# ACT's rounding of weight tiles is queued behind the evacuation three products back, and the two ends of the attention are reordered

## The chip, the core and the metric

The kernel runs on one core of one Trainium2 chip. PE is the matmul engine, with PEld its weight loads; DVE, ACT and POOL are the vector, scalar and GpSimd engines; SP issues nearly all DMAs. Each engine works through its own queue in the order in which the program was laid down for it. The metric is the device time of one execution in microseconds, lower is better.

## The reference, cut to what matters

Two decoder layers on 1040 tokens (16 learned ones ahead of 1024) of width 1024, all in float32. Layer 0 mixes by multi-head latent attention with 16 heads, layer 1 by a causal multi-scale pooling. Each mixer is followed by a gated MLP, and an RMS norm stands ahead of and behind every one of these.

```
for i in range(2):
    a = rmsnorm(h, norm_mix_pre[i])
    m = mla_mixer(a, ...) if i == 0 else pool_mixer(a, ...)
    h = h + rmsnorm(m, norm_mix_post[i])
    f = conv_ffn(rmsnorm(h, norm_ffn_pre[i]), w_up, conv_w, conv_b, w_down)
    h = h + rmsnorm(f, norm_ffn_post[i])
# conv_ffn: u = h @ w_up (1024 -> 5632); u = conv_b + causal width-3 depthwise conv of u;
#           gate, val = split(u); (silu(gate) * val) @ w_down (2816 -> 1024)
# attention: per block of 128 queries, causal softmax over the keys before it
```

## The kernel before

**Numbers.** Every matmul is done three times: each float32 operand is split into a rounded part ("hi") and the rest ("lo"), and hi·hi, lo·hi and hi·lo are summed in PSUM. `split` makes both: ACT rounds (`L64`, a CAST), DVE or POOL subtracts (`L70`). A weight tile is so loaded by SP (`L723`) into `wr`, of which there are 3; ACT writes `wh` and DVE `wl`, of which there are 4 each; then PE multiplies by both (`L764`). This is `wtile`, called once for every product.

**Attention.** Heads are worked through one by one, in three blocks of queries each (`b` = 0, 1, 2, with 3, 6 and 9 key tiles). While the `value_steps` of one block run (PE transposes the probabilities, ACT and DVE split them, PE multiplies by the values), `merge` lays the score tiles of the next block between them. `open_attention` prepares the first head's queries, keys and values; after that the scores of its first block are computed by themselves. The last block of the last head has no score tiles beside it. Each head's output goes to DRAM (`heads`) and comes back for the output projection.

**Dense part.** The tokens are split into two halves (536 and 504). For each half come `wo` (the output projection, 8 products), `ffn_up` (in two parts of 22 products each) and `ffn_down` (in two parts, 8 outputs of two products each: 6 and 5 of the 11 chunks of 128). A product lands in PSUM: room for 6 products of one bank for the second half, for 3 of two banks for the first. ACT then evacuates it: `evac` (`L773`) into a tile F in `wo` and the first part of `ffn_down`, the first tap of the convolution (`L908`) in `ffn_up`; in the second part of `ffn_down` DVE adds it to F, and ACT squares the sum. There are 8 tiles F. They hold the 8 outputs of one half until the norm behind them (`post`) has run: a column sum on PE (`L84`), a reciprocal root in some 13 small DVE instructions, a broadcast on PE (`L126`), a copy on ACT (`L130`), then DVE scales every F (`L833`) and adds it to the residual H (`L838`). Only this addition frees an F for the next half.

**Order.** The kernel is written as straight code; a scheduler simulates the engines and lays each engine's queue in the order in which it finds instructions ready. Norms and pooling of one half are generators (`self.bg`), advanced by `tick` between the products of the other half, with a priority 200 places ahead. In the pooling, each of 4 groups needs windowed sums on DVE, a rounding on ACT (`xh`, `L64`), a rest on DVE (`xl`) and a small product on PE.

Of the kernel before, what the change touches and what calls it, by code (L numbers as in the profile page):

```python
# [1 line left out]

# [1 line left out]

# [7 lines left out]
F32 = mybir.dt.float32  # L12
# [19 lines left out]
QT = 116  # L32
# [14 lines left out]
class Kern:  # L47
# [270 lines left out]
    def open_attention(self, es):  # L318

        tc = self.tc  # L320
        P = lambda name, bufs, **kw: es.enter_context(tc.tile_pool(name=name, bufs=bufs, reuse_waits="tile", **kw))
        self.ap = P("ap", 2)
        self.pss = P("pss", 2, space=PSUM)
        self.pst = P("pst", 2, space=PSUM)
        self.qt, self.vt, self.qr = {}, {}, {}
        self.avq, self.last_av = [], {}
        self.pps = [(self.psp, "pp"), (self.pst, "t"), (self.pss, "s")]
        self.mask = self.ap.tile([QT, 928], F32, name="mask", bufs=1)
        self.nc.sync.dma_start(self.mask, self.io["mask"])
        rs, ks, qs, vs = self.rope_steps(0), self.k_steps(0), self.q_steps(0), self.v_steps(0, 0, NQT)  # L330
        return [rs[0], ks[0], rs[1], qs[0], ks[1], *vs[:4], qs[1], rs[2], ks[2], qs[2], *vs[4:]]

    def pp(self, name):
        pool, tag = self.pps[0]
# [5 lines left out]
    def attention(self, es):  # L340
        tc, nc, io = self.tc, self.nc, self.io
        if True:
            P = lambda name, bufs, **kw: es.enter_context(tc.tile_pool(name=name, bufs=bufs, reuse_waits="tile", **kw))
            self.aq = P("aq", 2)
            self.pso = P("pso", 1, space=PSUM)

            self.pps = [(self.psp, "pp"), (self.pst, "t"), (self.pst, "t")]
            run = lambda steps: [st() for st in steps]
            blocks = [(h, b) for h in range(NH) for b in range(3)]
            P, steps = self.new_scores(0, 0)  # L350
            run(steps)
# [163 lines left out]

    def score_tile(self, h, b, i):

        nc, ap, sm = self.nc, self.ap, self.aq
# [4 lines left out]
        P = self.aq.tile([QT, min(T, 348 * (b + 1))], F32, tag=f"P{b}", name="P", bufs=3)  # L523
# [35 lines left out]
    def value_steps(self, h, b, P):  # L559
# [19 lines left out]
        def step(j):  # L579
            k0, kn = j * QT, min(QT, T - j * QT)  # L580
            pt = self.pp("ps_t")
            d = max(j - 3 * b, 0)
            for x in range(d, 3):
                Pi, n = P[x]
                nc.tensor.transpose(pt[:kn, x * QT:x * QT + n], Pi[:n, k0:k0 + kn], self.ident[:n, :n])  # L585
            th = self.aq.tile([QT, 348], F32R, tag="pth", name="pth", bufs=4)
            tl = self.aq.tile([QT, 348], F32R, tag="ptl", name="ptl", bufs=4)
            e0 = d * QT
            r0 = 0 if d == 0 else qn - 256
            if e0 > r0:  # L590
                nc.gpsimd.memset(th[:kn, r0:e0].bitcast(F32), 0.0)
                nc.gpsimd.memset(tl[:kn, r0:e0].bitcast(F32), 0.0)
            if j % self.PM == 1 and not (h == NH - 1 and b == 2):
                tf = self.aq.tile([QT, 348], F32, tag="ptf", name="ptf", bufs=1)
                nc.scalar.copy(tf[:kn, e0:qn], pt[:kn, e0:qn])
                self.split(tf[:kn, e0:qn], th[:kn, e0:qn], tl[:kn, e0:qn], hi_eng="pool")
            else:
                nc.scalar.copy(th[:kn, e0:qn], pt[:kn, e0:qn])  # L598
                nc.vector.tensor_tensor(tl[:kn, e0:qn], pt[:kn, e0:qn], th[:kn, e0:qn].bitcast(F32), op=ALU.subtract)  # L599
            self.avq.append(lambda: av(j, kn, r0, th, tl))  # L600
            while len(self.avq) > self.LAG:
                self.avq.pop(0)()
# [4 lines left out]
    def dense(self):  # L607
# [9 lines left out]
        self.H, self.A, self.bg = {}, {}, []  # L617

        F, acc = self.wo(0)
        self.bg.append(self.after_mixer(0, F, acc, 0, True))  # L620
# [86 lines left out]
        self.O[hf][0].append(hi)  # L707
        self.O[hf][1].append(lo)

    def wtile(self, src, nk, pool=False):  # L710
        nc = self.nc
        n = 128 * nk
        r = self.wp.tile([128, 1024], F32, tag="wr", name="wr", bufs=3)
        if pool:
# [6 lines left out]
        for i, a in enumerate(src):  # L721
            w = n // len(src)
            nc.sync.dma_start(r[:, i * w:i * w + w], a)  # L723
        self.split(r[:, :n], hi[:, :n], lo[:, :n], lo_eng="dve")
        return [(hi[:, 128 * k:128 * k + 128], lo[:, 128 * k:128 * k + 128]) for k in range(nk)]

    @staticmethod
# [40 lines left out]
    def evac(self, dst, ps, scale=None):  # L768
        c0 = 0
        for p in ps:  # L770
            d = dst[:, c0:c0 + p.shape[1]]
            if scale is None:
                self.nc.scalar.copy(d, p)  # L773
            else:
                self.nc.scalar.activation(d, p, AF.Copy, scale=scale)
            c0 += p.shape[1]

    def addsq(self, acc, t):

        nc, n = self.nc, t.shape[1]  # L780
        if acc is None:
            acc = self.tp.tile([128, HALF], F32, tag="acc", name="acc", bufs=2)[:, :n]
            nc.scalar.activation(acc, t, AF.Square)
        else:
            sq = self.tp.tile([128, HALF + 16], F32, tag="tc", name="sq")
            nc.scalar.activation(sq[:, :n], t, AF.Square)
# [4 lines left out]
    def wo(self, hf):  # L791
# [14 lines left out]
        for m in range(KD):  # L806
# [1 line left out]
                W, ps = early[m]  # L808
                self.mm_half(W[KD - 1:], *O, KD - 1, KD, ps)
            else:  # L810
                ps = self.mm_half(self.wtile(io["w_o"][m], KD), *O)
            if hf == 0:
                self.wo_load(1, m)
            f = self.fp.tile([128, HALF], F32, tag="F", name="F")[:, :HALVES[hf][1]]
            self.evac(f, ps)
            F.append(f)
            acc = self.addsq(acc, f)
            self.tick()
# [68 lines left out]
    def ffn_up(self, hf, part):  # L887
# [8 lines left out]
        for jj in range(JH):  # L896
            j = part * JH + jj
            cv = []
            for gv in range(2):
                idx = gv * NJ + j  # L900
                u, = self.mm_half(self.wtile(io["w_up"][L, j, :, gv], KD), ah, al, skip=skip)
                if (L, hf) == (0, 0):
                    t = self.up.tile([128, HALF], F32, tag="u", name="u")
                    nc.vector.tensor_tensor(t, u, self.late, op=ALU.mult)
                    u = t
                p0 = G_CONV + (L * 2 * NJ + idx) * 4
                c = self.tp.tile([128, HALF], F32, tag="t", name="cv")[:, :n]
                nc.scalar.activation(c, u[:, pad:pad + n], AF.Identity, bias=self.par(p0 + 3), scale=self.par(p0 + 2))  # L908
                for x in (1, 0):

                    o = max(0, 2 - x - pad)
# [15 lines left out]
    def ffn_down(self, part, G, F):  # L927
        nc, io, L = self.nc, self.io, self.L
        gh, gl = G
        out, acc = [], None  # L930
        src = lambda m, k0, nk: self.wtile(io["w_down"][L, part, m, :, k0:k0 + nk], nk)
        early = {}
        for m in range(2):
            early[m] = self.mm_half(src(m, 0, 6), gh, gl, 0, JH)
        for m in range(KD):
            ps = early[m] if m in early else self.mm_half(src(m, 0, 6), gh, gl, 0, JH)
            self.mm_half(src(m, 6, 5), gh, gl, 6, JH, ps)
            if F is None:
                f = self.fp.tile([128, HALF], F32, tag="F", name="F")[:, :gh[0].shape[1]]
                self.evac(f, ps)  # L940
            else:
                f = F[m]
                nc.vector.tensor_tensor(f, ps[0], f, op=ALU.add)
                acc = self.addsq(acc, f)
            out.append(f)
            self.tick()
        return out, acc
# [165 lines left out]
```

## Time and profile before

| | |
|---|---|
| Median of 3 runs | 2242.7 us (2241.12 to 2243.98) |
| The profiled execution, its own time | 2243.88 us |
| Its span from the first to the last instruction | 2242.1 us |
| Mean granted TensorE clock | 0.982 |
| PE busy | 2153.3 us, 96% of the span |
| DVE, ACT, POOL busy | 1466.7, 1045.3, 382.7 us (65%, 47%, 17%) |

The profile is of one execution. "Busy" is time in which the engine executed something; the clock is given as a share of full speed, of which the two levels are 2.4 GHz (1.0) and 1.2 GHz (0.5). Times such as 1143.75 are microseconds from the start of the span. By stages: the latents to about 105 us, attention to 547, output projection to 641, layer 0's MLP to about 1130, with the pooling of layer 1 beginning inside its second half, layer 1's MLP to the end.

### The profile page before, as it was taken

The page shows a single profiled execution, that of the slowest core. Times are in us where ns is not written, and L with a number is a line of the kernel's source. Part 1 is how long each engine was busy: PE and PEld are TensorE (multiplying, and loading weights), DVE is VectorE, ACT ScalarE, POOL GpSimd, SP SyncE. Part 2 cuts the span into 40 slices and gives each one's busy share as a digit, 9 for nine tenths or more (in the row PEclk, how much of TensorE's full clock was granted, in tenths as well). Part 3 has the DMA queues.
Part 4 walks back from the last instruction along what each step waited for, and adds up shares of the span by engine and source line. Part 5 has one row for each costly group of instructions (what it writes and reads, how often), then busy time and mean ns, then how long its engine had stood idle before and what let it go on. Part 6 is the DMA issues. An engine that isn't in the chain of part 4 may idle for free.

```text
span 2242.1 us, 36260 instructions
## 1 busy us (share of the span) xinstructions
PE 2153.3 (96%) x13890; PEld 1971.5 (88%) x13890; DVE 1466.7 (65%) x2713; ACT 1045.3 (47%) x1932; POOL 382.7 (17%) x728
## 2 busy tenths in 40 slices
PE   8889999998999999999998999999899999999996
PEld 8888888887989999999876888899899998888886
DVE  7877777776489726665877565587745557634656
ACT  6377777776464423433544344344434433433431
POOL 5567676764000000000000000000000000000001
PEclk9999999998999999999999999999999999999998
DMA  5011111114343232233322423422242244223231
GB/s 163 25 33 31 30 34 31 25 55 135 113 161 127 80 105 95 80 98 117 94 71 89 134 96 89 128 83 86 74 142 85 77 128 174 94 84 114 94 94 47
DMA packets 82901, 202.74 MB, mean 90 GB/s; under 512 B 10548, under 2 KB 31668, under 8 KB 82728
## 3 DMA queue, kind: packets, MB, share of 16 engines
q1 hardware_dynamic: 82584, 200.18, 28.7%
q8 instruction: 109, 1.79, 0.3%
q14 instruction: 64, 0.52, 0.1%
q10 hardware_dynamic: 144, 0.25, 0.0%
HBM read 179.15 MB, written 16.97 MB: 87 GB/s over the span
## 4 chain that ended last, share of the span: by engine, by line
PE 86%; DVE 5%; ACT 4%; DMA 2%; issue 2%; POOL 2%; DVEq 0%; SPq 0%; POOLq 0%; ACTq 0%
PE ps_m L764 72%; PE ps_t L585 2%; PE ps_s L534 2%; PE ps_o L570 1%; PE ps_s L535 1%; PE ps_s L536 1%; ACT P L548 1%; PE ps_o L571 1%; DMA xt<-in_x 1%; DVE ps_s L543 1%; PE ps_qk L415 1%; PE ps_qk L416 1%; PE ps_qk L417 1%; PE ps_st L84 1%; ACT pth L598 0%
## 5 line engine op out<-in xcount | busy, mean ns | idle before, releaser
L70 DVE TENSOR_TENSOR wl<-wr,wh 128x1024 fp32r<-128x1024 f32 (+3 forms) x316 | 348.4, 1103 | 416.0 <-ACT wh L64 406.8
L64 ACT CAST wh<-wr 128x1024 fp32r<-128x1024 f32 (+3 forms) x316 | 301.2, 953 | 590.3 <-PE ps_m L764 513.1
L764 PE MATMUL ps_m<-ah,wh 128*128 128x506 f32 (+2 forms) x2112 | 565.6, 322 | 3.7 <-DVE cv L912 2.0
L764 PE MATMUL ps_m<-al,wh 128*128 128x506 f32 (+2 forms) x2112 | 568.4, 323 | 0.0
L764 PE MATMUL ps_m<-ah,wl 128*128 128x506 f32 (+2 forms) x2112 | 565.1, 322 | 0.0
L764 PEld LDWEIGHTS ps_m<-ah,wh 128*128 128x128 f32 x2112 | 354.7, 190 | 34.6 <-ACT cv L908 2.2
L764 PEld LDWEIGHTS ps_m<-al,wh 128*128 128x128 f32 x2112 | 354.4, 190 | 27.7
L764 PEld LDWEIGHTS ps_m<-ah,wl 128*128 128x128 f32 x2112 | 354.5, 190 | 27.4
L764 PE MATMUL ps_m<-gh,wh 128*128 128x268 f32 (+3 forms) x1088 | 289.6, 319 | 2.2 <-ACT F L773 2.2
L764 PE MATMUL ps_m<-gl,wh 128*128 128x268 f32 (+3 forms) x1088 | 288.6, 318 | 0.0
L764 PE MATMUL ps_m<-gh,wl 128*128 128x268 f32 (+3 forms) x1088 | 288.5, 318 | 0.0
L912 DVE SCALAR_TENSOR_TENSOR cv<-ps_m,params,cv 128x504 f32<-128x504 f32 (+1 forms) x264 | 196.1, 744 | 3.1
L764 PEld LDWEIGHTS ps_m<-gh,wh 128*128 128x128 f32 x1088 | 184.0, 191 | 15.9 <-ACT F L773 2.4
L764 PEld LDWEIGHTS ps_m<-gh,wl 128*128 128x128 f32 x1088 | 182.9, 190 | 13.6
L764 PEld LDWEIGHTS ps_m<-gl,wh 128*128 128x128 f32 x1088 | 183.3, 190 | 13.1
L64 ACT CAST gh<-cv 128x504 fp32r<-128x504 f32 (+2 forms) x88 | 54.7, 622 | 170.3 <-DVE cv L918 170.3
L548 ACT ACTIVATE P<-ps_s,stat 116x116 f32<-116x116 f32 (+9 forms) x160 | 111.2, 698 | 31.9 <-DVE stat L543 25.0
L585 PE MATMUL ps_t<-ident,P 116*116 116x116 f32 x720 | 114.4, 268 | 11.5 <-DVE ptl L599 6.8
L916 ACT ACTIVATE cv<-cv 128x504 f32<-128x504 f32 (+2 forms) x88 | 55.9, 635 | 139.3 <-DVE cv L912 139.3
L553 POOL TENSOR_SCALAR P<-P,stat 116x116 f32<-116x116 f32 (+2 forms) x144 | 108.7, 757 | 57.5 <-DVE stat L551 49.8
L867 POOL TENSOR_SCALAR al<-ahalo 128x2 fp32r<-128x2 f32 x16 | 5.4, 336 | 631.6 <-PE ps_m L764 631.5
L585 PEld LDWEIGHTS ps_t<-ident,P 116*116 116x116 f32 x720 | 83.9, 136 | 25.8 <-DVE ptl L599 6.7
(201 smaller groups left out, 3605.5 us busy)
## 6 DMA issues: line engine op xcount, KB each, us to landing
wr<-in_w_up SPq DMA_DIRECT2D x176, 512.0 KB, 3.5
wr<-in_w_down SPq DMA_DIRECT2D x56, 384.0 KB, 3.1
wr<-in_w_down SPq DMA_DIRECT2D x56, 320.0 KB, 2.9
wr<-in_w_o SPq DMA_DIRECT2D x16, 512.0 KB, 3.6
resid<-H SPq DMA_DIRECT2D x16, 268.0 KB, 4.1
H<-resid SPq DMA_DIRECT2D x16, 268.0 KB, 3.4
xt<-in_x SPq DMA_DIRECT2D x32, 130.0 KB, 2.4
resid<-H SPq DMA_DIRECT2D x16, 252.0 KB, 3.9
```

The lines of the kernel that those rows point to most:

```text
L64: nc.scalar.copy(hi, src)
L70: eng.tensor_tensor(lo, src, hi.bitcast(F32), op=ALU.subtract)
L84: nc.tensor.matmul(ps[:w, i:i + 1], acc[:, w * i:w * i + w], self.ones, start=True, stop=True)
L415: nc.tensor.matmul(ps, wh, xh, start=i == 0, stop=False)
L416: nc.tensor.matmul(ps, wh, xl, start=False, stop=False)
L534: nc.tensor.matmul(ps[:n, x, :w], qh[:, qs], kh[:, ks], start=True, stop=False)
L548: nc.scalar.activation(dst, ps, AF.Exp, bias=mx[:n, 1:2], scale=-1.0, accum_out=es[:n, gi:gi + 1])
L553: nc.gpsimd.tensor_scalar(P[:n, :nk], P[:n, :nk], rs[:n], 1.0, op0=ALU.mult, op1=ALU.mult)
L585: nc.tensor.transpose(pt[:kn, x * QT:x * QT + n], Pi[:n, k0:k0 + kn], self.ident[:n, :n])
L764: nc.tensor.matmul(p, w, x[k][:, skip + c0:skip + c0 + m], start=k == 0 and w is wh and x is xh, stop=k == last and w is wl)
L912: nc.vector.scalar_tensor_tensor(c[:, o:], u[:, pad + x - 2 + o:pad + x - 2 + n], self.par(p0 + x), c[:, o:], op0=ALU.mult, op1=ALU.add)
L916: nc.scalar.activation(c, c, AF.Silu)
```

## The change

There are two independent parts.

**Weight tiles.** Every evacuation in the dense part is remembered in a list (`marks`). `wtile` takes a number, `behind`, and lays ACT's rounding of the tile into ACT's queue behind the evacuation that stands so many places back in the list. `issue_after` only orders instructions of one engine; it adds no wait of its own. The numbers are chosen so that the evacuation is that of the product three back, where that product has one (the first of the two products of an output of `ffn_down` has none, and the one before it is taken). In the second part of `ffn_down` the mark is ACT's square. Excepted are the first five tiles of the first half's `wo`, the pooling's tiles and the last `ffn_down`.

**Attention.** The three score tiles of the first head's first block are laid between the steps of `open_attention`; their probabilities and small statistics move to the pool that is open then. The last head's blocks run in the order 2, 1, 0 instead of 0, 1, 2. With that, the exception that keeps POOL out of the last block's splits moves from block 2 to block 0.

```
+        self.first, ss = self.new_scores(0, 0)
+        return [rs[0], ks[0], rs[1], qs[0], ks[1], ss[0], *vs[:2], ss[1], *vs[2:4], ss[2], qs[1],
+                rs[2], ks[2], qs[2], *vs[4:]]
...
-            blocks = [(h, b) for h in range(NH) for b in range(3)]
-            P, steps = self.new_scores(0, 0)
-            run(steps)
+            blocks = [(h, b) for h in range(NH - 1) for b in range(3)] + [(NH - 1, b) for b in (2, 1, 0)]
+            P = self.first
...
-            if j % self.PM == 1 and not (h == NH - 1 and b == 2):
+            if j % self.PM == 1 and not (h == NH - 1 and b == 0):
...
-    def wtile(self, src, nk, pool=False):
+    def wtile(self, src, nk, pool=False, behind=0):
+        order = self.tc.issue_after(self.marks[-behind]) if behind else nullcontext()
...
-        self.split(r[:, :n], hi[:, :n], lo[:, :n], lo_eng="dve")
+        with order:
+            self.split(r[:, :n], hi[:, :n], lo[:, :n], lo_eng="dve")
...
-                ps = self.mm_half(self.wtile(io["w_o"][m], KD), *O)
+                ps = self.mm_half(self.wtile(io["w_o"][m], KD, behind=3 if hf or m > 4 else 0), *O)
...
-            self.evac(f, ps)
+            self.marks.append(self.evac(f, ps))
...
-                u, = self.mm_half(self.wtile(io["w_up"][L, j, :, gv], KD), ah, al, skip=skip)
+                W = self.wtile(io["w_up"][L, j, :, gv], KD, behind=2 if jj + gv == 0 else 3)
+                u, = self.mm_half(W, ah, al, skip=skip)
...
+                self.marks.append(getattr(i, "ins", i))
...
-            early[m] = self.mm_half(src(m, 0, 6), gh, gl, 0, JH)
+            early[m] = self.mm_half(src(m, 0, 6, 3 - m), gh, gl, 0, JH)
...
-            ps = early[m] if m in early else self.mm_half(src(m, 0, 6), gh, gl, 0, JH)
-            self.mm_half(src(m, 6, 5), gh, gl, 6, JH, ps)
+            ps = early[m] if m in early else self.mm_half(src(m, 0, 6, 3 if m == 2 else 2), gh, gl, 0, JH)
+            self.mm_half(src(m, 6, 5, 1 if m == 0 else 2), gh, gl, 6, JH, ps)
```

## Rows read from the trace of the kernel before

**Rows 1.** The page, busy time (share of the span) and instructions by engine.
```profile
PE 2153.3 (96%) x13890; PEld 1971.5 (88%) x13890; DVE 1466.7 (65%) x2713; ACT 1045.3 (47%) x1932; POOL 382.7 (17%) x728
```

**Rows 2.** Busy by stage: stage, length, PE, PEld, DVE, ACT, POOL, clock, DMA, GB/s.
```profile
655.00:1143.00 488.00, 488.00 (x3598) 470.56 (x3598) 327.93 (x483) 201.73 (x272) 6.29 (x24) 1.00 0.32 102
1143.00:1200.00 57.00, 42.46 (x193) 35.44 (x192) 43.20 (x73) 22.98 (x41) 1.66 (x8) 0.85 0.17 50
```

**Rows 3.** PE's waits, whole span: us in total, times, longest.
```profile
PE ps_m L764 <- ACT xh L64: 17.2, 4, 10.1
...
PE ps_m L764 <- ACT F L773: 3.6, 2, 2.2
```

**Rows 4.** ACT's waits from 562 to 2200 us.
```profile
ACT wh L64 <- PE ps_m L764: 513.1, 272, 6.0
```

**Rows 5.** DVE's waits from 562 to 2200 us.
```profile
DVE wl L70 <- ACT wh L64: 403.0, 213, 4.6
```

**Rows 6.** Timeline of ACT in the pooling: start, us, instruction, idle before it.
```profile
1143.75 1.04 ACT L64 CAST wh<-wr 128x1024 fp32r<-128x1024 f32 x1 [3.77 <-PE ps_m L764]
...
1145.87 0.64 ACT L64 CAST xh<-pmx 128x536 fp32r<-128x536 f32 x1
```

**Rows 7.** Timeline of PE, second half of the output projection.
```profile
603.32 1.08 PE L84 MATMUL ps_st<-ones,acc 128*67 128x1 f32 x16
...
612.60 0.41 PE L126 MATMUL ps_bc<-diag,ones_r 67*128 67x268 f32 x2
...
613.79 0.39 PE L764 MATMUL ps_m<-oh,wh 128*128 128x504 f32 x1
```

**Rows 8.** Timeline of DVE over the same stretch.
```profile
598.05 0.72 DVE L787 TENSOR_TENSOR acc<-acc,sq 128x536 f32<-128x536 f32 x1
...
619.62 0.71 DVE L838 TENSOR_TENSOR H<-H,F 128x536 f32<-128x536 f32 x1
620.24 1.22 DVE L70 TENSOR_TENSOR wl<-wr,wh 128x1024 fp32r<-128x1024 f32 x1
```

**Rows 9.** Timeline of ACT over the same stretch.
```profile
620.36 0.58 ACT L773 COPY F<-ps_m 128x504 f32<-128x504 f32 x1
```

**Rows 10.** Timeline of PE, `ffn_down` of layer 0, second half, first part.
```profile
1215.73 0.40 PE L764 MATMUL ps_m<-gh,wh 128*128 128x504 f32 x1
...
1217.35 0.66 PE L126 MATMUL ps_bc<-diag,ones_r 67*128 67x268 f32 x4
```

**Rows 11.** Timeline of ACT over the same stretch.
```profile
1225.43 0.56 ACT L773 COPY F<-ps_m 128x504 f32<-128x504 f32 x1
```

**Rows 12.** Timeline of PE, `ffn_down` of layer 1, first half, first part.
```profile
1615.65 0.40 PE L764 MATMUL ps_m<-gh,wh 128*128 128x260 f32 x2
...
1621.65 0.74 PE L764 MATMUL ps_m<-gh,wh 128*128 128x260 f32 x2 [2.23 <-ACT F L773]
```

**Rows 13.** Timeline of ACT over the same stretch.
```profile
1621.03 0.57 ACT L773 COPY F<-ps_m 128x520 f32<-128x520 f32 x1
```

**Rows 14.** Busy time by 5 us behind PE's longest wait; columns as in rows 2.
```profile
1190.00:1195.00 5.00, 4.87 (x14) 4.06 (x15) 3.94 (x8) 0.71 (x2) 0.00 (x0) 0.50 0.00 0
```

**Rows 15.** Timeline of ACT, layer 0's MLP, first half.
```profile
699.30 1.05 ACT L64 CAST wh<-wr 128x1024 fp32r<-128x1024 f32 x1 [2.09 <-PE ps_m L764]
...
708.20 0.84 ACT L908 ACTIVATE cv<-u,params 128x536 f32<-128x536 f32 x1 [1.37 <-DVE u L904]
```

**Rows 16.** PE's waits from 100 to 128 us.
```profile
PE ps_s L534 <- ACT P L548: 1.6, 2, 1.2
PE ps_t L585 <- POOL P L553: 1.3, 2, 1.0
```

**Rows 17.** Busy time of the attention's end; columns as in rows 2.
```profile
520.00:546.00 26.00, 19.39 (x106) 16.07 (x103) 19.86 (x38) 18.74 (x44) 12.21 (x28) 0.81 0.55 174
```

**Rows 18.** The chain that ended last, attention's end: start, us, what.
```profile
537.61 4.47 DMA heads<-o
542.21 2.74 DMA or<-heads
```

More of the change, by code (lines that the diff above doesn't have):

```diff
@@ L1 @@
-from contextlib import ExitStack
+from contextlib import ExitStack, nullcontext
 import numpy as np
@@ L330, in open_attention @@
         rs, ks, qs, vs = self.rope_steps(0), self.k_steps(0), self.q_steps(0), self.v_steps(0, 0, NQT)
-        return [rs[0], ks[0], rs[1], qs[0], ks[1], *vs[:4], qs[1], rs[2], ks[2], qs[2], *vs[4:]]
+        self.first, ss = self.new_scores(0, 0)
+        return [rs[0], ks[0], rs[1], qs[0], ks[1], ss[0], *vs[:2], ss[1], *vs[2:4], ss[2], qs[1],
+                rs[2], ks[2], qs[2], *vs[4:]]
     def pp(self, name):
@@ L516, in score_tile @@
     def score_tile(self, h, b, i):
-        nc, ap, sm = self.nc, self.ap, self.aq
+        nc, sm = self.nc, self.ap
         qh, ql = self.qt[h]
@@ L522, in score_tile @@
         groups = self.KCH[i]
-        P = self.aq.tile([QT, min(T, 348 * (b + 1))], F32, tag=f"P{b}", name="P", bufs=3)
+        P = (self.aq if b else self.ap).tile([QT, min(T, 348 * (b + 1))], F32, tag=f"P{b}", name="P", bufs=3)
         stat = sm.tile([QT, 8], F32, tag="st", name="stat", bufs=4)
@@ L616, in dense @@
         self.dtile = lambda x: self.tp.tile([128, HALF], F32R, tag="x" + x, name="diag", bufs=2)
-        self.H, self.A, self.bg = {}, {}, []
+        self.H, self.A, self.bg, self.marks = {}, {}, [], []
         F, acc = self.wo(0)
@@ L772, in evac @@
             if scale is None:
-                self.nc.scalar.copy(d, p)
+                i = self.nc.scalar.copy(d, p)
             else:
-                self.nc.scalar.activation(d, p, AF.Copy, scale=scale)
+                i = self.nc.scalar.activation(d, p, AF.Copy, scale=scale)
             c0 += p.shape[1]
+        return getattr(i, "ins", i)
     def addsq(self, acc, t):
@@ L782, in addsq @@
             acc = self.tp.tile([128, HALF], F32, tag="acc", name="acc", bufs=2)[:, :n]
-            nc.scalar.activation(acc, t, AF.Square)
+            i = nc.scalar.activation(acc, t, AF.Square)
+            self.squared = getattr(i, "ins", i)
         else:
             sq = self.tp.tile([128, HALF + 16], F32, tag="tc", name="sq")
-            nc.scalar.activation(sq[:, :n], t, AF.Square)
+            i = nc.scalar.activation(sq[:, :n], t, AF.Square)
+            self.squared = getattr(i, "ins", i)
             i = nc.vector.tensor_tensor(acc, acc, sq[:, :n], op=ALU.add)
@@ L907, in ffn_up @@
                 c = self.tp.tile([128, HALF], F32, tag="t", name="cv")[:, :n]
-                nc.scalar.activation(c, u[:, pad:pad + n], AF.Identity, bias=self.par(p0 + 3), scale=self.par(p0 + 2))
+                i = nc.scalar.activation(c, u[:, pad:pad + n], AF.Identity, bias=self.par(p0 + 3),
+                                         scale=self.par(p0 + 2))
+                self.marks.append(getattr(i, "ins", i))
                 for x in (1, 0):
@@ L930, in ffn_down @@
         out, acc = [], None
-        src = lambda m, k0, nk: self.wtile(io["w_down"][L, part, m, :, k0:k0 + nk], nk)
+        src = lambda m, k0, nk, b: self.wtile(io["w_down"][L, part, m, :, k0:k0 + nk], nk, behind=b)
         early = {}
         for m in range(2):
-            early[m] = self.mm_half(src(m, 0, 6), gh, gl, 0, JH)
+            early[m] = self.mm_half(src(m, 0, 6, 3 - m), gh, gl, 0, JH)
         for m in range(KD):
-            ps = early[m] if m in early else self.mm_half(src(m, 0, 6), gh, gl, 0, JH)
-            self.mm_half(src(m, 6, 5), gh, gl, 6, JH, ps)
+            ps = early[m] if m in early else self.mm_half(src(m, 0, 6, 3 if m == 2 else 2), gh, gl, 0, JH)
+            self.mm_half(src(m, 6, 5, 1 if m == 0 else 2), gh, gl, 6, JH, ps)
             if F is None:
                 f = self.fp.tile([128, HALF], F32, tag="F", name="F")[:, :gh[0].shape[1]]
-                self.evac(f, ps)
+                mark = self.evac(f, ps)
             else:
@@ L944, in ffn_down @@
                 acc = self.addsq(acc, f)
+                mark = self.squared
+            self.marks.append(mark)
             out.append(f)
```

## The prediction

> **What bounds the kernel now.** The page comes first: PE is busy 2153 of 2242 us [rows 1], so the reader looks for the some 90 us in which it is not, and in which stages they lie. The view by stages says where: from 655 to 1143 us PE has no gap at all and the full clock, while from 1143 to 1200, where the first pooling is mixed into the MLP, it is busy 42.5 of 57 us at a mean clock of 0.85 [rows 2]. PE's waits name what ends last there: four waits for ACT's `xh`, 17.2 us, the longest 10.1; in the dense part next to it only two waits for an evacuation into F, 3.6 us [rows 3]. The rest lies at the attention's two ends [rows 16, 17].
>
> Then the two engines that serve PE. ACT waits 272 times, 513 us in all, at the head of its queue with a rounding of a weight tile whose slot PE still reads [rows 4], and DVE 213 times, 403 us, with the rest of that tile behind it [rows 5]. Where PE is saturated that costs nothing. In the pooling it does: a rounding of 1.04 us, for which ACT stood still 3.77, runs ahead of the `xh` on which PE waits [rows 6]. That is what the new order can give back.
>
> What it can take is seen in the timeline of the output projection's second half. The first evacuation into F starts at 620.36 [rows 9], 0.03 us behind the end of the first addition F+H on DVE, 619.62 + 0.71 [rows 8]: it waits for a free F. PE by then is in its fifth product; its fourth began at 613.79 [rows 7]. So PE today runs ahead of ACT's evacuations by as many products as PSUM has room for, since the weights come without regard to them.
>
> **The change, part by part.** *Start of the attention.* No work is added; three score tiles are moved ahead. Beside it PE waits 1.6 us for their exponents and 1.3 for their scaling before the first transposes [rows 16]. Laid between the projections both can be hidden: 2.9 us is the gain at most, and the loss at most the same if the tiles only push the last norm, on DVE, by as much. I take -2.5, as each of the waits is for one link of a chain that now starts earlier.
>
> *End of the attention.* From 520 to 546 us PE is busy 19.4 of 26 us at a clock of 0.81 [rows 17]: 6.6 us of gaps and at most 0.19 x 26 = 4.9 us of slow clock, 11.5 in all. The last block has 9 steps with no scores beside them; with the order 2, 1, 0 it has 3. Two thirds of 11.5 are 7.7; I take -7.5, with bounds of 0 (the rounding of the first weights and of `heads` on ACT and DVE fills the time) and -11.5. What moves along: the output of the last block, needed by the projection's eighth chunk, now leaves last. Its way through DRAM is 4.47 + 2.74 us [rows 18], with a rounding and a rest some 9. The projection starts with 3 products of 7 chunks, 126 matmuls of 268 columns. From the end of the column sum at 604.4 to 613.79 PE did 39 matmuls of 504 columns and a broadcast of some 0.5 us [rows 7], 0.23 us each, so 0.12 for 268: 15 us, which covers that way with 6 to spare. SP's queue is passed too: the later weight tiles queue behind this load, and have the same cover.
>
> *The rounding moves behind an evacuation: gains.* The instructions stay the same, 316 of them; DMAs stay where they are. Where `xh` is waited for, one rounding less stands ahead of it, 4 x 1.04 = 4.2 us [rows 3, 6]; DVE no longer meets the rest of a tile too early, which is worth one mean wait of 403/213 = 1.9 us ahead of the longest gap [rows 5]. I take -6; the bounds are 0 and -20, the four waits and a clock that does not fall.
>
> *The same move: the hold.* A tile now cannot be rounded before the product three back is evacuated. Where evacuations follow at once, two products lie between, and hide a rounding of 1.04 and a rest of 1.22 us [rows 6, 8]. Where F is short, the hold takes PE's lead away. Three places have that.
>
> 1. Output projection, second half. The fourth tile stands behind the first evacuation: 620.36 + 0.58 + 1.04 + 1.22 = 623.2, against a start at 613.79. The first two matmuls can go ahead (-0.5), and the chain of the norm begins 1 us earlier, since no rounding stands ahead of the last F of the first half: 7.9. Behind the longest wait PE ran a 5 us stretch at a clock of 0.50 [rows 14], so a wait of this kind costs 2.4 more. The 1.4 us for F that PE waits at its end today (3.6 less the 2.23 of place 3) go: +8.9.
> 2. `ffn_down` of layer 0, second half. The third output's second tile stands behind the first evacuation, now at 1225.43 [rows 11]. The broadcast at 1217.35 can go when PE runs dry, at 1215.73, 1.6 us earlier [rows 10]. With 0.56 for the evacuation and, by five eighths of the rows above, 0.65 and 0.76 for the tile, it is ready at 1225.8, against 1215.73; less 0.5, less 0.7 for the broadcast, less 1 as in place 1: 7.9, with the clock +10.3.
> 3. `ffn_down` of layer 1, first half: evacuation at 1621.03 [rows 13], tile ready at 1623.0, against 1615.65 less 0.5: 6.9. PE today waits 2.23 a little later for the same evacuation [rows 12]: +4.6, and the clock has fallen in both.
>
> The sum is +23.8. Its bounds: the norm's column sum starts at 603.32, though its input is there at 598.77 [rows 7, 8]. If PE, running dry, took that and the broadcast (the same delay, an estimate from this one) at once, places 1 and 2 would shrink by 9 each, and place 3 to nothing: +2. If nothing comes earlier, the rests wait behind additions of DVE, and the clock falls thrice: +32. I take the value near the rows, because both norm matmuls lie ahead of the fourth product already, where PE does not run dry.
>
> A rule of the Trainium skill speaks here. First the row: PE is in its fifth product before the first is evacuated [rows 7, 9]. The page "Perfetto Trace Analysis" (section "Matmul Optimizations") asks that all PSUM banks be used, to have as much independent work in flight as there is room for. By that rule the hold, which leaves three products in flight where there is room for six, loses; without it the sum below would be 16 us under the time of before, with it 8 above.
>
> *Where evacuation itself is late.* In layer 0's MLP, first half, the product that ended at about 699.3 meets its first tap at 708.20, since DVE is busy with the norm [rows 15]. 708.2 + 0.84 + 1.04 + 1.22 = 711.3, and two products of 24 x 0.23 x 536/504 = 5.9 us each end at 711.1. I take 0; the bound is +4, one more such queue on DVE.
>
> **Sum.** 2243.9 (the profiled execution) - 2.5 - 7.5 - 6 + 23.8 = 2251.7. That execution lies 1.2 us above the median of the runs, 2242.7, so 2250.5.
>
> **Rivals.** *The hold is cheap (opposite sign).* Everything is as above, but the norm's matmuls move up where PE runs dry, and the hold costs 2: 2243.9 - 16 + 2 - 1.2 = 2228.7. For it: 4.5 us between a ready input and PE's start on it. Against: PE's queue has an order that is laid beforehand, and those matmuls stand ahead of the dry place already. It decides from a hold under 11.5 us on.
>
> *They cancel.* A hold of 11.5 to 20.5 us lands within 0.2% of before, 4.5 us, which is about what a measurement of this kernel can tell from no change: 2243.
>
> *The late way through DRAM is not covered.* If the weight tiles that queue on SP behind the last load of `heads` come after the 15 us of cover, the attention's end gives nothing: 2258. Against: the 6 us that it has to spare.
>
> *The new order of roundings changes nothing*, because ACT's evacuations stood ahead of them in most places anyway: the attention's 10 us remain, 2232.7. Against: the 272 waits [rows 4].
>
> **Chances.** The forecast 0.45, DRAM way 0.08, both slower: 0.53. Cancelling 0.15. Cheap hold 0.27 and no effect 0.05, both faster: 0.32. The likeliest case's own range is 2243 to 2263. The range for 8 in 10 must take in cases of both signs: it reaches down to the cheap hold less some 3 us, 2226, and up to 2262, which leaves out some 0.1 at either end.
>
> **What would show it.** Right: in PE's waits, the rest `wl` appears as releaser, at three places, about 8, 8 and 7 us long, at the fourth product of the projection's second half and at the third output of two `ffn_down`; ACT's waits with a rounding for PE shrink from 513 us to near none; the pooling's waits for `xh` shrink by some 1 us each; and from 520 us to the projection's start 7 us are gone. Wrong: no wait of PE for `wl` over 3 us there, or a longer wait at the projection's eighth chunk. The forecast falls if the scheduler lays the norm's column sum and broadcast at least 4 us earlier against PE's products.

## The result, and the profile after

The changed kernel takes 2274.5 us (median of four executions, 2271.87 to 2276.54) where the kernel before, beside it on the same chip, takes 2242.6 (2241.12 to 2243.98). The ratio is 1.0138, interval 1.0126 to 1.0151: slower by 31.9 us. The forecast was slower by 7.8, so the side is right and the size is off by 24. The profiled execution is the shortest of the four, 2271.87, with a span of 2269.9 us against 2242.1. The two traces that are compared below therefore differ by 27.8 us and not by 31.9: the one of before lies 1.2 us above its median, the one of after 2.6 below.

The page of the kernel after, busy time and three of its groups (busy, mean ns, idle time before and what ended it):

```profile
PE 2157.4 (95%) x13890; PEld 1971.8 (87%) x13890; DVE 1457.5 (64%) x2711; ACT 1034.4 (46%) x1932; POOL 386.8 (17%) x732
...
L70 DVE TENSOR_TENSOR wl<-wr,wh 128x1024 fp32r<-128x1024 f32 (+3 forms) x316 | 343.6, 1099 | 184.9 <-ACT wh L64 177.3
...
L64 ACT CAST wh<-wr 128x1024 fp32r<-128x1024 f32 (+3 forms) x316 | 293.5, 945 | 51.1 <-PE ps_m L770 37.5
```

The instructions are nearly the same in number and length as before. The change did what it says: ACT's waits at the head of its queue with a rounding, 513.1 us before [rows 4], are 37.5, and DVE's with a rest fell from 403.0 [rows 5] to 172.3 (562 to 2230 us, the same stages). Nearly all of that idle time cost nothing, and its end brought nothing; ACT now idles ahead of the evacuations instead (415 us for PE, in `cv` and F). PE's waits, after, whole span:

```profile
PE ps_m L770 <- ACT wh L64: 28.9, 8, 9.1
PE ps_m L770 <- ACT xh L64: 18.3, 3, 11.8
...
PE ps_m L770 <- ACT F L779: 1.8, 2, 1.7
```

The first line is new: eight waits for a rounded weight. The second answers to [rows 3], where it was 17.2 in four. The timeline of PE says where they lie (start, us, instruction, idle before it):

```profile
562.69 0.39 PE L770 MATMUL ps_m<-oh,wh 128*128 128x268 f32 x1 [1.66 <-ACT F L779]
...
619.69 0.79 PE L770 MATMUL ps_m<-oh,wh 128*128 128x504 f32 x1 [9.07 <-ACT wh L64]
...
622.80 0.79 PE L770 MATMUL ps_m<-oh,wh 128*128 128x504 f32 x1 [1.90 <-ACT wh L64]
...
1177.07 1.26 PE L770 MATMUL ps_m<-xh,pwh 128*128 128x268 f32 x4 [3.90 <-ACT xh L64]
...
1199.05 1.26 PE L770 MATMUL ps_m<-xh,pwh 128*128 128x268 f32 x4 [11.81 <-ACT xh L64]
...
1233.97 0.79 PE L770 MATMUL ps_m<-gh,wh 128*128 128x504 f32 x1 [8.66 <-ACT wh L64]
...
1643.42 0.80 PE L770 MATMUL ps_m<-gh,wh 128*128 128x260 f32 x2 [4.90 <-ACT wh L64]
```

These are the three places of the forecast: the projection's second half, and the first part of `ffn_down` in layer 0's second half and in layer 1's first.

To say what each stage costs, the start of the same product is read in both timelines, and the difference (after minus before) is followed through the program. A stage's price is what is added in it.

| at the start of (us) | before | after | difference | added since the line above |
|---|---|---|---|---|
| the first products of queries and keys | 88.67 | 88.41 | -0.3 | |
| the value products halfway | 351.27 | 347.24 | -4.0 | start of the attention: -3.8 |
| the projection's second half | 595.77 | 592.46 | -3.3 | end of the attention and first half: +0.7 |
| layer 0, `ffn_up` | 642.94 | 653.77 | +10.8 | place 1: +14.1, the 1.4 of F gone, 20 norm matmuls more |
| layer 0, first `ffn_down` | 777.85 | 787.35 | +9.5 | those 20 norm matmuls, behind the line above in before: -1.3 |
| layer 0, second half, `ffn_down` | 1191.18 | 1200.11 | +8.9 | first pooling: -0.6 |
| its second part, `ffn_up` | 1259.10 | 1281.31 | +22.2 | place 2: +13.3 |
| layer 1, first half, `ffn_down` | 1591.48 | 1614.13 | +22.7 | second pooling: +0.4 |
| its second part, `ffn_up` | 1664.35 | 1692.45 | +28.1 | place 3: +5.5 |
| the last `ffn_down` | 2160.89 | 2189.05 | +28.2 | +0.1 |

In place 1 the 1.4 us that PE waited for F before are gone; on the other side the column sum and the broadcast of the second half's norm, 20 matmuls of some 1.4 us, stand ahead of the line in the trace of after and behind it in that of before. So place 1 costs 14.1 - 1.3 = 12.8 net.

The hold is 12.8 + 13.3 + 5.5 = 31.6 us, forecast 23.8. The gains are 3.8 - 0.7 + 0.2 = 3.3, forecast 16.

### The profile page after: what moved, and what is told of

It is laid out like the page before. It is cut to its first block, busy times and chain, and to the rows that moved or that the text cites. A ratio compares the mean times of both kernels' runs of the same rounds, so it can differ in the third digit from the quotient of the medians.

```text
span 2269.9 us, 36299 instructions
## 1 busy us (share of the span) xinstructions
PE 2157.4 (95%) x13890; PEld 1971.8 (87%) x13890; DVE 1457.5 (64%) x2711; ACT 1034.4 (46%) x1932; POOL 386.8 (17%) x732
## 3 DMA queue, kind: packets, MB, share of 16 engines
q1 hardware_dynamic: 82584, 200.18, 27.8%
q8 instruction: 109, 1.79, 0.3%
## 4 chain that ended last, share of the span: by engine, by line
PE 84%; DVE 7%; ACT 3%; issue 2%; POOL 2%; DMA 2%; SPq 0%; DVEq 0%; POOLq 0%; ACTq 0%
PE ps_m L770 70%; PE ps_t L587 2%; PE ps_s L536 2%; PE ps_o L572 1%; PE ps_o L573 1%; PE ps_s L538 1%; PE ps_s L537 1%; ACT P L550 1%; DVE ps_s L545 1%; DVE F L842 1%; PE ps_qk L417 1%; PE ps_qk L418 1%; PE ps_qk L419 1%; PE ps_st L84 0%; PE ps_d L232 0%
## 5 line engine op out<-in xcount | busy, mean ns | idle before, releaser
L70 DVE TENSOR_TENSOR wl<-wr,wh 128x1024 fp32r<-128x1024 f32 (+3 forms) x316 | 343.6, 1099 | 184.9 <-ACT wh L64 177.3
L770 PEld LDWEIGHTS ps_m<-ah,wh 128*128 128x128 f32 x2112 | 354.2, 190 | 33.6 <-ACT wh L64 2.0
L64 ACT CAST wh<-wr 128x1024 fp32r<-128x1024 f32 (+3 forms) x316 | 293.5, 945 | 51.1 <-PE ps_m L770 37.5
L918 ACT ACTIVATE cv<-ps_m,params 128x504 f32<-128x504 f32 (+1 forms) x132 | 102.5, 777 | 244.3 <-PE ps_m L770 244.3
L770 PEld LDWEIGHTS ps_m<-gl,wh 128*128 128x128 f32 x1088 | 184.5, 191 | 13.3
L550 ACT ACTIVATE P<-ps_s,stat 116x812 f32<-116x812 f32 (+9 forms) x160 | 111.4, 698 | 34.2 <-DVE stat L545 25.3
L779 ACT COPY F<-ps_m 128x504 f32<-128x504 f32 (+3 forms) x56 | 28.6, 531 | 177.2 <-PE ps_m L770 170.8
```

The costliest lines, as they stand in the source:

```text
L64: nc.scalar.copy(hi, src)
L70: eng.tensor_tensor(lo, src, hi.bitcast(F32), op=ALU.subtract)
L550: nc.scalar.activation(dst, ps, AF.Exp, bias=mx[:n, 1:2], scale=-1.0, accum_out=es[:n, gi:gi + 1])
L770: nc.tensor.matmul(p, w, x[k][:, skip + c0:skip + c0 + m], start=k == 0 and w is wh and x is xh, stop=k == last and w is wl)
L779: i = self.nc.scalar.copy(d, p)
L918: i = nc.scalar.activation(c, u[:, pad:pad + n], AF.Identity, bias=self.par(p0 + 3), scale=self.par(p0 + 2))
```

## Place 1, read closely

DVE, after, while PE is dry (PE's last broadcast of the norm starts at 610.21):

```profile
611.24 5.59 DVE L842 SCALAR_TENSOR_TENSOR F<-F,params,R 128x536 f32<-128x536 f32 x8 [5.87 <-ACT R L130]
616.74 5.10 DVE L847 TENSOR_TENSOR H<-H,F 128x536 f32<-128x536 f32 x8
621.76 0.77 DVE L884 SCALAR_TENSOR_TENSOR al<-H,params,ah 128x536 fp32r<-128x536 f32 x1
622.45 1.22 DVE L70 TENSOR_TENSOR wl<-wr,wh 128x1024 fp32r<-128x1024 f32 x1
```

ACT over the same stretch:

```profile
617.49 0.58 ACT L779 COPY F<-ps_m 128x504 f32<-128x504 f32 x1 [6.28 <-DVE H L847]
617.96 0.74 ACT L883 ACTIVATE ah<-H,params 128x536 fp32r<-128x536 f32 x1
618.61 1.03 ACT L64 CAST wh<-wr 128x1024 fp32r<-128x1024 f32 x1
```

All eight scalings run ahead of the first addition, so the first F is free only at 617.45; the evacuation follows, then the norm's `ah`, and then the rounding. The rest of that tile is ready at 623.67, because it stands behind all eight additions and one `al`. (PE's second wait, which ends at 622.80, is for the fifth tile's rounding: the fifth product's first two matmuls stand in PE's queue ahead of the fourth's first one with the rest. Without them PE would have waited for that rest.) Before, the rest came right behind the first addition [rows 8], since its rounding had been done long before.

The forecast had the tile ready at 623.2, less 1 for an earlier norm, which is 618.9 on this trace's time (less 3.3). It is 4.8 later: the norm's column sum starts 0.5 later and not 1 earlier (600.47 against 603.32 - 3.3), so the evacuation comes 1.4 late; 0.65 for `ah`; 2.8 for the rest behind the additions. And PE then runs at the lower clock. Windows of 5 us, after, columns as in [rows 2]:

```profile
620.00:625.00 5.00, 3.10 (x7) 1.80 (x7) 5.00 (x7) 5.00 (x9) 0.00 (x0) 0.50 0.91 324
625.00:630.00 5.00, 5.00 (x19) 4.01 (x19) 5.00 (x8) 5.00 (x10) 0.00 (x0) 0.78 0.70 238
630.00:635.00 5.00, 5.00 (x23) 4.11 (x22) 5.00 (x8) 4.40 (x9) 0.00 (x0) 1.00 0.21 75
```

Place 1 is thus 9.07 + 1.90 = 11.0 us of waits, less the 1.4 for F that it had before, and what is left of the 12.8, 3.2, is put down to the clock (granted 0.50, that is 1.2 GHz, until about 627); place 2 is 9.6 of waits (8.66, 0.54, 0.40) and 3.7; place 3 is 5.6 of waits (4.90, 0.50, 0.16) and 2.1, less the 2.2 for F that it had before.

## The experiments

Theory H: the loss is the tie at the three places where F is short, and the attention gives little. Against it stood that the attention's own gain is there and is eaten (A), that the tie costs or gains elsewhere too (D), and that the tie itself counts and not how far back it reaches (E).

**The attention alone.** No rounding is tied.

```
-        order = self.tc.issue_after(self.marks[-behind]) if behind else nullcontext()
+        order = nullcontext()
```

> Both attention parts, and no rounding tied to an evacuation. Theory H (the loss is the hold at three places, the attention gives little): the changed kernel's trace shows the attention 4.0 us ahead before its last blocks and 3.3 ahead at the start of the output projection's second half, so about 2243 - 3.3 = 2239 us, and no wait of PE for a rounded weight over 2 us. Rival A (the reordered attention's own gain is 10 us, as forecast, and is lost to the held roundings in the projection's first half): 2233. Rival B (the attention part itself costs something later): over 2245.

2240.9 us against 2242.5, ratio 0.9996 (0.9987 to 1.0004). Both rivals fall: A's 2233 and B's 2245 lie outside. Of H's 3.3 us the medians show 1.6, and the interval takes in no change at all.

**The roundings alone**, with the attention of before.

> The roundings behind the evacuations, with the attention as it was before. Theory H: the three places cost 12.8, 13.0 and 5.6 us by the positions of equal products in the two traces, 31.4 in all, so 2243 + 31 = 2274 us, with PE's waits for ACT's rounding of about 9 + 2, 9 and 5 us at the same three places. Rival A: the same 31. Rival C (the hold is as dear as forecast, 24 us, and the rest of the loss comes from the two parts meeting): 2267.

2276.1 us, ratio 1.0150 (1.0135 to 1.0166). PE's waits for a rounded weight, whole span:

```profile
PE ps_m L769 <- ACT wh L64: 27.4, 7, 9.1
```

The three places cost 14.0 (13.0 net), 11.8 and 4.9. C's 2267 falls. The parts add up: +33.6 - 1.6 = 32.0, measured together 31.9.

**The three places free.** Everything else stays tied.

```
-  behind=3 if hf or m > 4 else 0)
+  behind=3 if not hf and m > 4 else 0)
...
-  src = lambda m, k0, nk, b: self.wtile(..., behind=b)
+  src = lambda m, k0, nk, b: self.wtile(..., behind=b if F else 0)
```

> The changed kernel, but the roundings of the output projection's second half and of the first part of each ffn_down are not tied to an evacuation; all others stay tied. Theory H: the loss is gone whole, 2239 us, the same as with the attention alone. Rival D (the order costs in the other places too, in the pooling or the convolution, or it gains there the 6 us that were forecast for the pooling): it differs from the attention alone by more than 4 us, 2233 with the gain.

2243.4 us, ratio 1.0004 (0.9996 to 1.0013). The same line of PE's waits:

```profile
PE ps_m L770 <- ACT wh L64: 3.2, 2, 1.8
```

The loss is gone whole. Against the attention alone it is 2.5 us longer, so the 6 us of gain elsewhere (D) are not there; in the trace the poolings add 0.7 and 2.2.

**One product looser.** One mark further back at the three places.

```
-  behind=3 if hf or m > 4 else 0)
+  behind=4 if hf else 3 if m > 4 else 0)
...
-  src = lambda m, k0, nk, b: self.wtile(..., behind=b)
+  src = lambda m, k0, nk, b: self.wtile(..., behind=b + (F is None))
```

> The changed kernel, but at the three places the rounding stands one mark further back: behind the evacuation four products back in the projection, one output (two products) further back in ffn_down. Theory H (the stall is the time by which PE's lead is short, so a product more of lead takes its length off): the projection's product of 24 matmuls of 0.23 us is 5.5 us, so its wait of 11.0 falls to about 5.5; an output of ffn_down is 33 matmuls, 7.6 us, so the waits of 9.6 and 5.6 us fall to about 2 and 0. With the clock some 20 us come back: 2254. Rival E (what counts is that ACT's rounding is tied at all, not how far back): about 2274, waits unchanged.

2270.8 us, ratio 1.0124 (1.0109 to 1.0139), much less than expected: the interval overlaps that of the changed kernel (1.0126 to 1.0151), so the time alone does not show a gain. PE's timeline at place 1:

```profile
623.84 0.50 PE L770 MATMUL ps_m<-oh,wh 128*128 128x504 f32 x1 [3.55 <-ACT wh L64]
...
626.95 0.79 PE L770 MATMUL ps_m<-oh,wh 128*128 128x504 f32 x1 [2.38 <-ACT wh L64]
```

There the dose is as expected: 9.07 became 3.55, one product of 5.5 us, and the place's price fell by 5. In `ffn_down` my expectation was wrong: one mark further back moves the stall to the next product, five chunks or 15 matmuls of 0.23, 3.5 us, and not by an output; the waits fell from 9.6 to 8.1 and from 5.6 to 3.4, less even than those 3.5, which is not explained. The three places together came down from 31.6 to 22.4. Of these 9 us the new order took 6 back: 3.4 in the projection's first half (a wait of 3.29 for an evacuation) and 2.5 in the second pooling (a wait of 6.79 for DVE). E falls at place 1, by the trace.

**Scalings and additions in pairs**, in the changed kernel.

```
+  with self.tc.issue_after(i) if k else nullcontext():
       nc.vector.scalar_tensor_tensor(F[k], F[k], self.par(gcol + k), R, op0=ALU.mult, op1=ALU.mult)
...
-  nc.vector.tensor_tensor(h, h, F[k], op=ALU.add)
+  i = nc.vector.tensor_tensor(h, h, F[k], op=ALU.add)
```

> The changed kernel, with DVE's scalings and additions of a norm in pairs: each scaling of F is laid behind the addition of the F before it, so the first F is free after one scaling and one addition and not after eight scalings and one addition. Theory H1 (the hold lasts until that first addition): the first F comes free 7 x 0.7 = 4.9 us earlier at each of the three places; the waits of 11.0, 9.6 and 5.6 us fall to about 6, 5 and 1, and with a clock that falls for less time 16 us come back: 2258. Rival E (the hold is the tie itself, or the rest on DVE that stands behind all additions): 2270 or more.

2253.3 us beside 2243.4 for before, ratio 1.0045 (1.0032 to 1.0059): of 31.9 us 22 come back, and E falls. DVE and then PE at place 1:

```profile
612.80 0.78 DVE L843 SCALAR_TENSOR_TENSOR F<-F,params,R 128x536 f32<-128x536 f32 x1 [5.86 <-ACT R L130]
613.61 0.72 DVE L848 TENSOR_TENSOR H<-H,F 128x536 f32<-128x536 f32 x1
...
618.37 1.22 DVE L70 TENSOR_TENSOR wl<-wr,wh 128x1024 fp32r<-128x1024 f32 x1
```

```profile
616.56 0.79 PE L770 MATMUL ps_m<-oh,wh 128*128 128x504 f32 x1 [4.38 <-ACT wh L64]
...
619.64 0.79 PE L770 MATMUL ps_m<-oh,wl 128*128 128x504 f32 x1 [1.87 <-DVE wl L70]
```

The first F is free 1.5 us behind the start of the scalings and not 6.2. The waits at the three places are 6.3, 4.0 and 0.5 (expected 6, 5 and 1), their prices 7.6, 7.2 and -2.8 us, 12 in all against 31.6. The way to the first addition is thus what sizes most of the hold. Another 3.6 us come back in the second pooling.

**The start alone, and the end alone.**

```
-  blocks = [(h, b) for h in range(NH - 1) for b in range(3)] + [(NH - 1, b) for b in (2, 1, 0)]
+  blocks = [(h, b) for h in range(NH) for b in range(3)]
```

That is the start alone, with the exception for POOL back at block 2; the end alone keeps the order 2, 1, 0 and takes the start's lines of the diff back. No rounding is tied in either.

> Only the score tiles of the first head's first block laid between the projections; the last head in its old order, no rounding tied. Theory H: in three traces the attention runs 3.7 us ahead of before from the second head on, counted from the stage ahead of it, and this is all that the attention gives: 2242.5 - 3.7 = 2239 us, the lead unchanged to the end. Rival A (the gain was to come from the end): within 1 us of 2242.

2242.1 against 2243.4, ratio 0.9992 (0.9983 to 1.0001). In the trace the start gives 3.9 us, of which 2 are left at the projection's second half. So H's "unchanged to the end" fails, and the time is the one that A gave; A's reason, a gain from the end, is refuted by the next run.

> Only the last head's blocks in the order 2, 1, 0, with the exception for POOL moved; no rounding tied. Theory H: the reordered end brings the projection some 1.5 us forward, and the projection's first half gives 2 back, since its fourth product waits for an evacuation that stands behind roundings of heads which come through DRAM no earlier than before: 2242.5 + 0.5 = 2243 us. Rival A (the forecast's 7.5 us): 2235.

2247.6, ratio 1.0019 (1.0010 to 1.0028): slower by 4.2, more than expected; A's 2235 falls. In the trace the attention's end and the projection's first half add 2.1; 1.8 more were there before the last head, where this kernel differs in nothing, and are not explained. The first pooling adds 2.1 (a wait of 6.08 for `xh` where 1.79 stood), and place 3 gives 1.5 back.

**Why the end gives nothing: three tries.** In the first, each rounding of `heads` for the second half is laid behind the evacuation beside it, and its load comes behind that evacuation in the program (both attention parts, no weight tied).

```
+  with self.tc.issue_after(self.marks[-1]) if hf else nullcontext():
       self.split(r[:, :n], hi, lo, lo_eng="dve")
```

> Both attention parts, no rounding of a weight tied; but each head's rounding for the projection's second half (oh, on ACT) is laid behind the evacuation of the product beside it. Theory H (the end's gain is given back because the evacuations of the projection's first products stand behind roundings of heads that wait for DRAM): PE's wait for an evacuation at the fourth product, 1.3 us in the run of the attention alone, goes, and the projection's second half starts some 2 us earlier against the attention's last full block; about 2240.5 - 2 = 2238.5 us. Rival F (the projection's first half is paced by the loads themselves, so a later wait takes its place): 2240 to 2242.

2249.2 us, ratio 1.0027 (1.0017 to 1.0036), 8 longer than without. The wait for the evacuation is gone, and a wait of 4.93 for the fourth weight tile has come: weights and `heads` share the three buffers `wr`, so a later rounding holds a buffer longer (SP asks for that tile at 565.59, when the first held rounding, of 564.22, is over). H is not borne out as the cure.

> The end alone (2, 1, 0), with POOL kept off the splits of block 2 of the last head as well as of block 0. Theory P (the gaps at the end stay because block 2, with the most steps, now has POOL's slower splits in its chain, where it had none before): the 2 us that the projection's second half starts late in the run of the end alone turn into a lead of 2 or more: 2243 us or less against 2247. Rival G (each of the three short blocks ends in a chain of its own, copy and addition of an output, whoever splits): within 2 us of the end alone.

2249.0, ratio 1.0027 (1.0016 to 1.0037). It was one line, `b != 1` for `b == 0` in the exception. P falls; the time is G's. Still, in the trace the last head gets quicker by 2.1 us (its last wait for an output ends at 540.15, at 545.06 in the end alone, of which 2.8 were there before). But the projection begins no sooner. PE, then SP's queue in the same run:

```profile
546.58 0.82 PE L769 MATMUL ps_m<-oh,wh 128*128 128x268 f32 x2 [5.38 <-ACT wh L64]
```

```profile
524.45 1.54 SPq L704 DMA_DIRECT2D or<-heads  x3
533.36 0.45 SPq L578 DMA_DIRECT2D heads<-o  x1
534.90 4.93 SPq L704 DMA_DIRECT2D or<-heads  x4
540.12 0.45 SPq L578 DMA_DIRECT2D heads<-o  x1
540.75 0.96 SPq L727 DMA_DIRECT2D wr<-in_w_o  x2
```

The projection's first weights are asked for at 540.75, behind seven loads of `heads`; in the changed kernel at 534.43, and the first is rounded at 538.53, where before it was at 537.84, though the attention ran 4 us ahead. (The late projection is not all of the loss here: 3.3 us more come in the first pooling, with a wait of 6.07 for `xh` as in the end alone.) I blamed the writes of outputs between the loads, and moved them.

```
-  nc.sync.dma_start(self.io["o"][...], o[:, :qn])
+  (nc.gpsimd if h == NH - 1 else nc.sync).dma_start(self.io["o"][...], o[:, :qn])
```

> As the end without POOL, but the three output writes of the last head are issued by POOL and not by SP. Theory Q (the end gives nothing because SP's queue is served in order: in the run before this one the loads of the earlier heads and then of the projection's first weights stand behind the write of block 2's output, 533.36, and of block 1's, 540.12, which wait for their blocks to end): seven loads of heads and three of weights follow one another from 524.5 on, at some 1.4 us each with three slots the first weights land 5 us or more sooner than 545.4, PE's wait of 5.4 us for the first rounded weight goes, and 2249 falls to 2244 or less. Rival R (the transfers themselves, or the three slots and the roundings that free them, set the pace): the wait stays over 4 us, 2247 or more.

2250.8, ratio 1.0036 (1.0022 to 1.0050). Theory Q falls:

```profile
524.90 15.77 SPq L704 DMA_DIRECT2D or<-heads  x7
541.59 3.33 SPq L727 DMA_DIRECT2D wr<-in_w_o  x3
```

With nothing between them the seven loads still take 16 us, since the fourth needs one of the three buffers, and ACT rounds the first only at 533.62. The wait for the first weight is 4.24. So R holds, the buffers and the roundings that free them. ACT comes to that rounding so late because it is at work: it is busy 8.55 of the 9.57 us from 524.05 to 533.62, with the last head's exponents and casts, which stand ahead in its queue. No run moved the rounding forward.

**The start and the pairs, nothing tied, the old end.**

> The kernel before, with the start of the attention reordered and the scalings and additions in pairs; no rounding tied, the last head in its old order. Theory H1: the two waits for a free F (1.4 and 2.2 us) go as well, so 2242.5 - 3.7 - 3.6 = 2235 us. Rival E (the pairs cost DVE more than they free, since each scaling now waits for the addition before it): 2239 or more, the same as the start alone.

2231.3 us, ratio 0.9947 (0.9934 to 0.9959): 12 us faster than before and 11 faster than the start alone (2242.1), so E falls and the pairs bring nearly all of it. Of the two waits for F the longer is gone and the 1.4 stays; that gives 4.1 us. More came from the poolings' stretches, 4.5 and 3.7 us by the trace, which the expectation did not have. In the trace of before two waits stood there that are gone:

```profile
1146.57 0.76 PE L764 MATMUL ps_m<-xh,pwh 128*128 128x268 f32 x4 [2.62 <-ACT xh L64]
...
1473.48 0.48 PE L764 MATMUL ps_m<-ah,wh 128*128 128x260 f32 x2 [1.99 <-DVE cv L912]
```

The other three waits for `xh` stay: 1.79, 10.12 and 2.67, the last now under DVE's name. Each of the three waits that went had a slow clock behind it, 0.66 to 0.73 over 5 us, and takes some 2 us more with it than its own length.

**And the pooling's sums on POOL.**

```
-  acc = self.addsq(acc, f)
+  acc = self.addsq(acc, f, nc.gpsimd)
```

> The start and the pairs, as in the run that was 12 us faster than before, and the pooling's sums of squares, 8 additions of 0.71 us on DVE in each half, are made by POOL, which is nearly idle there. Theory D (the pooling's long waits of PE for the rounded pooled tokens, xh, come from DVE, which is full there, and not from ACT's roundings of weights ahead of them): the longest wait of 10.1 us shrinks by the two additions that lie in its chain and by those ahead of it, 2 to 5 us, in the first pooling, and some 2 in the second: 2226 to 2229 us. Rival I (ACT's order sets these waits, as the forecast of -6 took it): 2231, waits unchanged.

2229.6 us, ratio 0.9942 (0.9928 to 0.9956), the shortest here, yet not to be told from the 2231.3. The long wait did not shrink, 11.97 us in one. DVE ahead of it, and POOL beside it:

```profile
1173.83 1.83 DVE L1043 SCALAR_TENSOR_TENSOR pa<-H,params,R 128x536 f32<-128x536 f32 x1
...
1176.93 3.38 DVE L1053 TENSOR_TENSOR psm<-psm 128x549 f32<-128x549 f32 x3
...
1180.97 0.77 DVE L1043 SCALAR_TENSOR_TENSOR pa<-H,params,R 128x536 f32<-128x536 f32 x1
```

```profile
1173.74 1.34 POOL L796 TENSOR_TENSOR acc<-acc,sq 128x536 f32<-128x536 f32 x1 [6.02 <-ACT sq L794]
...
1176.28 1.78 POOL L796 TENSOR_TENSOR acc<-acc,sq 128x536 f32<-128x536 f32 x1
```

While POOL adds, the same DVE instruction takes 1.83 us that takes 0.77 alone, and three sums take 3.38 (2.24 in the trace of before). DVE lost some 2.2 us where it was to save 1.4. So D was not tested cleanly by this, and I is not shown either.

## Why the forecast was wrong, point by point

The forecast was +7.8 us, these traces show +28.2 at the last product. Of the 20.4 between them the attention's end has 8.2, the hold 7.8 and the roundings out of the way 5.8; the start took 1.3 off.

- **The hold (+23.8; measured 31.6): right in mechanism and place, too small.** The step that failed here is "I take the value near the rows" between the bounds 2 and 32. It lies at the upper end, with just what stood there: the norm's column sum comes no earlier, the rests stand behind DVE's additions, the clock falls thrice. Waits: 26.1 us against 7.9 + 7.9 + 6.9 = 22.7. Clock: 3.2 + 3.7 + 2.1 = 9.0 against 2.4 + 2.4. Subtracted for what goes: 3.6 (1.4 + 2.2), as forecast. The 1 us for an earlier norm, in places 1 and 2, was not there. The sign that the forecast named, waits for `wl` of about 8, 8 and 7 us, did not come: the longest is 0.40. A held product's first matmul already needs `wh`, so the long waits end with the rounding itself.
- **Roundings out of the way (-6; measured -0.2).** The step that failed is "one rounding less stands ahead of it, 4 x 1.04": the term with the wrong cause. With the three places free the poolings gained nothing. Ahead of the longest wait ACT stands idle for DVE, before and after:

```profile
1189.43 0.64 ACT L64 CAST xh<-pmx 128x536 fp32r<-128x536 f32 x1 [6.30 <-DVE pmx L1044]
```

```profile
1198.36 0.64 ACT L64 CAST xh<-pmx 128x536 fp32r<-128x536 f32 x1 [3.64 <-DVE pmx L1058]
```

  [rows 6] show only the first of the four waits, where a rounding did stand ahead, and I took it for all. The two short waits it may have helped, 2.62 and 1.79, became one of 3.90.
- **The attention's end (-7.5; measured +0.7).** The step that failed is "two thirds of 11.5": it counted steps, where what counts at the end is when seven chunks of `heads` and the first weights have come through three buffers. The rival of the way through DRAM was near, though not by the queue that it named: the projection's first three products had their cover, but ACT's evacuation of the first (562.25) stood behind a rounding of `heads` that waited for its load, hence the wait of 1.66 at 562.69. ACT, after:

```profile
560.67 0.61 ACT L64 CAST oh<-or 128x504 fp32r<-128x504 f32 x1 [3.25 <-DMA or<-heads]
561.19 1.04 ACT L64 CAST wh<-wr 128x1024 fp32r<-128x1024 f32 x1
562.25 1.81 ACT L779 COPY F<-ps_m 128x268 f32<-128x268 f32 x6
```

  By the start of the projection's steady run the end had given 1.1 us; this wait took 1.8 back.
- **The attention's start (-2.5; measured -3.8 in this trace, -2.4 to -3.9 in the others that have it).** The bound of 2.9 was too narrow; it counted two waits and no clock (granted 0.84 from 120 to 130 us before, 1.00 after). In the times no more than 1.6 us of the attention as a whole can be seen.
- **The late evacuation (0, bound +4).** Right: the difference between the traces goes up and down by about 1 us around 711 and is back at +9.5 from 749 to 1038.
- **The rivals.** The cheap hold fell: at place 1 the broadcast stayed at the end of the third product, 4.4 us behind its input. No rival had the hold above 24 and the gains near 0 at once. These three errors point one way, which is why the range (up to 2262) missed: the terms were summed as if each could miss on either side, but the end and the roundings came out at the bound of 0 that the forecast itself had given them, and the loss at its upper bound of 32.

The rule of the Trainium skill cited in the prediction ("Perfetto Trace Analysis", section "Matmul Optimizations": all PSUM banks in use) agrees with the trace in direction: a product more of lead took 5.5 us off the first wait at place 1 (9.07 to 3.55). How many banks are needed no run here shows.

## What to carry to other kernels

An engine's long idle time at the head of its queue was no cost here as long as the engine behind it was ahead; tying a producer to a consumer's progress removes that lead, and the price shows where the consumer's buffer comes free late. Size such a stall by everything queued ahead of the freed buffer and behind it, to the last input of the first product, and add the clock behind the wait. If a buffer is freed by the second of two passes over eight tiles, do both per tile: that order on DVE took 11 us off the kernel with the reordered start.

## What was not expected of the hardware

POOL can hold DVE up: a DVE instruction of 0.77 us took 1.83 beside an addition on POOL. The Trainium skill names what may be the reason in "Perfetto Trace Analysis", section "Optimizing Scalar/DVE Operations": the two share an SBUF read port, so moving work between them might not help. The trace agrees with the second half, with these numbers; that the port is the reason, no run here shows. Also, the stage before the attention, which no kernel here changes, ends between 0.3 us sooner and 1.9 later than in the trace of before (by the first products of queries and keys), so positions in two traces are compared from a stage's own start.
